# Stick-breaking stage of a two-layer decoder trunk: TensorE in program order, longer step distances, an output projection begun with one half of its inputs

## The chip, the cores and the metric

The kernel runs on one core of one Trainium2 chip. The time is the device time of one execution in microseconds (us), the median of several runs. The kernel before takes 1203.66 us (three runs, 1200.4 to 1204.41).

## The reference

`x` is 256 tokens of 1024 features in float32. Two layers each do four updates of `x`: a half-weighted SwiGLU, a token mixer, cross-attention into 256 memory tokens, and a second half-weighted SwiGLU, each behind an RMS norm. The mixer of the even layer has two kinds of heads whose outputs are concatenated and projected:

```
x = x + 0.5 * swiglu_ffn(rms_norm(x, ...), ...)
h = rms_norm(x, mix_norm[layer])
x = x + even_mixer(h, ...)      # layer 0:  [banded heads | stick-breaking heads] @ w_out
x = x + odd_mixer(h, ...)       # layer 1
x = x + memory_cross_attention(rms_norm(x, ...), rms_norm(mem, ...), ...)
x = x + 0.5 * swiglu_ffn(rms_norm(x, ...), ...)
```

Stick-breaking attention, for each of 8 heads of 64 features, over keys `s` before token `t`:

```
z = q . k * dh**-0.5
log_keep  = where(strict, log_sigmoid(-z), 0)
log_after = cumsum(log_keep, reverse) - log_keep
a = where(strict, exp(log_sigmoid(z) + log_after), 0)
o = a @ v
```

## The kernel before, in words

Nearly all of the work is float32 matrix products, each made as three products of float32r parts: an operand is split into a high part and the rest, and `mm3` (lines 182 to 184) issues high x high, high x low and low x high. A weight tile (128 x 1024) is loaded by SyncE's queue into one of 4 buffers `raw`; ScalarE casts it to `wh` (line 175), VectorE subtracts to `wl` (line 177), 10 buffers of each. `project` (line 266) makes a product with 1024 output features: for the first 128 tokens (t = 0) it runs over the 8 slices k of the weights with both column halves c, then for t = 1 over c and k. One `step` of it is one `mm3` of 512 columns, so three matmuls, and calls `tick(650)`.

Small work is put between those steps by hand. `later(delay, fn, tag)` puts a function into a heap with a due time on a planning clock (in ns, line 92); every `tick` advances the clock and then calls at most one function that is due; `need(tag)` (line 108) calls functions in order of due time until none with that tag is left. The delays stand in the table `LAG` (line 30). The recorded program is then given to a list scheduler, which sets the order on each engine by a cost model of its own, except under `tc.manual_schedule(engines=...)`, where the engines named keep the order of the program.

Around the change, in `even_mixer` (line 547): after the banded heads, `mem.keys()` (a `project` of the memory tokens) runs on TensorE, and the steps of the stick-breaking heads are meant to stand between its matmuls. For head h:

- `stick` (line 699): for each second head the scores of two heads (lines 705 and 708, 64 rows of the array each), masks (713, VectorE); then ScalarE 716, 717, 718, VectorE 722, ScalarE 724 (high part), VectorE 725 (low part) and 727.
- `after` (732), due `stick_u` later: three matmuls that make the running sums (734 with the high part, 735 with the low part, 736), called a triple below; then VectorE 738, ScalarE 739.
- `values` (746), due `stick_v` later, for two heads: four groups of matmuls of line 496. After heads 3 and 7 a split (line 190 on ScalarE, 191 on VectorE) puts the outputs into `xh`, `xl`, the left operand of the output projection.

`need("stick")` then empties the heap, and the last `project` (line 772) multiplies by `w_out`. Its slices k = 0 to 3 need the banded heads alone, k = 4, 5 heads 0 to 3 and k = 6, 7 heads 4 to 7. `head256` (519) makes normed, transposed queries and keys of the cross-attention, with a transpose (`tp`, line 212) due `head256` after the scaling (452 or 536). In the cross-attention `attend` scales the probabilities (452) and has them transposed `x_p` later.

Of the kernel before, what the change touches and what calls it, by code (L numbers as in the profile page):

```python
# [18 lines left out]
P = 128  # L19
S = 256  # L20
D = 1024
NK = D // P
# [5 lines left out]


LAG = {  # L30
    "norm": 5000, "silu": 5000, "pv": 3000, "head256": 2200, "band": 7500, "band_gap": 2600, "band_p": 7500,
    "put": 400, "att_norm": 4500, "band_norm": 3500, "stick_gap": 1900, "stick_u": 3200, "stick_v": 1000, "stick_o": 1300, "head64": 7000,
    "att_first": 3800, "att_gap": 3300, "att_p": 17600, "att_o": 1800, "x_s": 18000, "x_p": 4000, "x_out": 3600,
    "mem_e": 5400, "mem_o": 4600, "rs64": 2700, "rs256": 1900, "rsband": 6100,
}

# [2 lines left out]
def kernel(  # L39
# [52 lines left out]
    def later(delay, fn, tag=None):  # L92
        serial[0] += 1
        heapq.heappush(heap, (clock[0] + delay, serial[0], tag, fn))
# [8 lines left out]
    def tick(ns):  # L103
        clock[0] += ns
        if heap and not busy[0] and heap[0][0] <= clock[0]:
            dispatch()

    def need(tag):
        while any(e[2] == tag for e in heap):
            dispatch()  # L110
# [32 lines left out]
    xh, xl = xs[:, 0], xs[:, 1]  # L143
# [22 lines left out]
    def weights(src, r=None, kept=False):  # L166
        if r is None:
            r = raw.tile([P, 1024], F32, name="raw")
        if len(src.shape) == 4:
            for g in range(2):  # L170
                nc.sync.dma_start(r.rearrange("p (k g n) -> p k g n", g=2, n=src.shape[3])[:, :, g, :], src[:, :, g, :])
        else:
            (kept_load if kept else nc.sync.dma_start)(r if len(src.shape) == 2 else blocks(r, src.shape[2]), src)
        wh = wsp.tile([P, 1024], F32R, name="wh")
        nc.scalar.copy(wh, r)  # L175
        wl = wsp.tile([P, 1024], F32R, name="wl")
        nc.vector.tensor_tensor(wl, r, f32(wh), op=ALU.subtract)  # L177
        return wh, wl
# [10 lines left out]
    def split_to(dh, dl, src):  # L189
        nc.scalar.copy(dh, src)  # L190
        nc.vector.tensor_tensor(dl, src, f32(dh), op=ALU.subtract)  # L191
# [45 lines left out]
    def announce(vec, kept=False):  # L237
        upcoming["gain"] = None if vec is None else load_gain(vec, kept)
# [11 lines left out]
    def add_to_x(scale):  # L250
        def evac(t, c, ps):
            xs = xres[t][:, c * 512:(c + 1) * 512]
            if scale == 1.0:
                nc.vector.tensor_tensor(xs, ps, xs, op=ALU.add)
            else:
                nc.vector.scalar_tensor_tensor(xs, in0=ps, scalar=scale, in1=xs, op0=ALU.mult, op1=ALU.add)
            x_updated(t, c)
        return evac
# [4 lines left out]
    def xboth(k):  # L263
        return xh[:, :, k, :], xl[:, :, k, :]

    def project(view, lhs, evac, nk=NK, tags=(None, None)):

        head = nk - 8
        ps = [[None, None], [None, None]]

        def step(t, c, k, w):
            if k == 0:
                ps[t][c] = psum()
            mm3(ps[t][c], lhs(t, k), cols(w, c * 512, 512), k == 0, k == nk - 1)
            tick(650)

        for k in range(head):
            w = weights(view(k))
            for t in range(2):
                for c in range(2):  # L280
                    step(t, c, k, w)
        if tags[0]:
            need(tags[0])
        ws = []
        for k in range(head, nk):
            ws.append(weights(view(k)))
            for c in range(2):
                step(0, c, k, ws[-1])
        for c in range(2):
            evac(0, c, ps[0][c])  # L290
        if tags[1]:
            need(tags[1])
        for c in range(2):
            for k in range(head, nk):
                step(1, c, k, ws[k - head])
            evac(1, c, ps[1][c])
# [250 lines left out]
    def even_mixer(w_in, q_gain, k_gain, sinks, w_out, next_vec, mem, first=False):  # L547
# [141 lines left out]
        need("band")  # L689

        for t in range(2):
            later(LAG['put'] + 1000 * t, lambda t=t: split_to(xh[:, t, 0:4, :], xl[:, t, 0:4, :], oA[:, t]), f"o{t}")

        po = [None]

# [3 lines left out]
        def stick(h):  # L699
            b = h // 2  # L700
            if h % 2 == 0:
                two = [psum(), psum()]
                rows = [slice(0, 64), slice(64, 128)]
                for ps, hs in zip(two, rows):
                    nc.tensor.matmul(ps.rearrange("p (a t) -> p a t", t=256)[:, :, 0:128],  # L705
                                     lhsT=kbT[hs, b, 0:P], rhs=qbT[hs, b, :], start=True, stop=False)
                for ps, hs in zip(two, rows):
                    nc.tensor.matmul(ps[:, 128:256], lhsT=kbT[hs, b, P:2 * P], rhs=qbT[hs, b, P:2 * P],
                                     start=False, stop=True)
                tick(800)  # L710
                for i in range(2):
                    zs[i] = work()
                    nc.vector.tensor_tensor(zs[i][:, 0:384], two[i][:, 0:384], smask, op=ALU.add)  # L713
            z = zs[h % 2][:, 0:384]
            e = work()
            nc.scalar.activation(e[:, 0:384], z, AF.Abs)
            nc.scalar.activation(e[:, 0:384], e[:, 0:384], AF.Exp, scale=-1.0)
            nc.scalar.activation(e[:, 0:384], e[:, 0:384], AF.Ln, bias=1.0)
            sp = work()
            sph = work(F32R)  # L720
            spl = work(F32R)
            nc.vector.scalar_tensor_tensor(sp[:, 0:384], in0=z, scalar=0.0, in1=e[:, 0:384],
                                           op0=ALU.max, op1=ALU.add)
            nc.scalar.copy(sph[:, 0:384], sp[:, 0:384])
            nc.vector.tensor_tensor(spl[:, 0:384], sp[:, 0:384], f32(sph[:, 0:384]), op=ALU.subtract)
            a = work()
            nc.vector.scalar_tensor_tensor(a[:, 0:384], in0=z, scalar=0.0, in1=e[:, 0:384],
                                           op0=ALU.min, op1=ALU.subtract)
            if h < 7:
                later(LAG['stick_gap'], lambda: stick(h + 1), "stick")  # L730

            def after():
                pc = psum()
                nc.tensor.matmul(pc[:, 0:384], lhsT=neg_ur, rhs=sph[:, 0:384], start=True, stop=False)
                nc.tensor.matmul(pc[:, 0:384], lhsT=neg_ur, rhs=spl[:, 0:384], start=False, stop=False)
                nc.tensor.matmul(pc[:, 256:384], lhsT=neg_1, rhs=sp[:, 128:256], start=False, stop=True)
                tick(540)
                nc.vector.tensor_tensor(a[:, 0:384], pc[:, 0:384], a[:, 0:384], op=ALU.add)
                nc.scalar.activation(a[:, 0:384], a[:, 0:384], AF.Exp)

                weighed[h % 2] = a.rearrange("p (b n) -> p b n", n=P)
                if h % 2 == 0:
                    return
                both = list(weighed)

                def values():
                    if h % 4 == 1:
                        po[0] = blocks(psum())
                    b = (h // 2) % 2
                    pair = (h - 1, h)  # L750

                    def vs(kb):
                        return lambda g: vb[:, kb, g * 64:(g + 1) * 64]
                    value_pairs(lambda g: po[0][:, 2 * b:2 * b + 2, :], pair, vs(0),
                                lambda g: both[g % 2][:, 0:3:2, :], True, False)
                    value_pairs(lambda g: po[0][:, 2 * b + 1, :], pair, vs(1),
                                lambda g: both[g % 2][:, 1, :], False, True)
                    tick(660)
                    if h % 4 == 3:
                        o = po[0]  # L760
                        b4 = 4 + 2 * (h // 4)
                        later(LAG['stick_o'], lambda: split_to(
                            *[x[:, :, b4:b4 + 2, :].rearrange("p t f n -> p f t n") for x in (xh, xl)],
                            o.rearrange("p (f t) n -> p f t n", f=2)), "o0")
                later(LAG['stick_v'], values, "stick")
            later(LAG['stick_u'], after, "stick")

        later(0, lambda: stick(0), "stick")
        mem.keys()
        need("stick")  # L770
        announce(next_vec)
        project(lambda k: w_out[k * P:(k + 1) * P, :], xparts, add_to_x(1.0), tags=("o0", "o1"))


    def odd_mixer(w_in, q_gain, k_gain, w_out, next_vec, mem):
# [278 lines left out]
```

## Time and profile before

| | us |
|---|---|
| median of three runs | 1203.66 |
| the profiled execution | 1202.92 |
| its span, first to last instruction | 1201.2 |
| TensorE busy, 99% of the span | 1189.3 |
| VectorE busy, 65% | 775.1 |
| ScalarE busy, 54% | 646.5 |

TensorE is busy nearly all the time, and 93% of the chain that ended last is its own. A matmul's busy time is longer than its turn in the queue, because matmuls overlap; what one costs is the distance from its start to the start of the next. In the timeline the first column is the start in us from the start of the span, the second the time until the end of the last of the merged instructions.

### The profile page before, as it was taken

What the parts mean: (1) busy time and instruction counts of PE and PEld (TensorE: products, weight loads), DVE (VectorE), ACT (ScalarE), POOL (GpSimd) and SP (SyncE); (2) the same over time, 40 slices, a digit from 0 to 9 for tenths busy, and PEclk for the clock granted to TensorE, in tenths of its full rate; (3) what the DMA queues carried; (4) which work ended last, traced back from release to release, by engine and by line L of the source; (5) the groups of instructions that cost most, each with busy time, mean ns of one, the idle gap of its engine ahead of it and who ended that gap; (6) DMA issues with size and microseconds to landing.
All of it is one profiled execution on the core that took longest, in us unless ns stands there. A gap on an engine that the chain in (4) does not pass through costs nothing.

```text
span 1201.2 us, 16964 instructions
## 1 busy us (share of the span) xinstructions
PE 1189.3 (99%) x6320; PEld 998.7 (83%) x6320; DVE 775.1 (65%) x1026; ACT 646.5 (54%) x1080; POOL 63.9 (5%) x123
## 2 busy tenths in 40 slices
PE   8999999999999999999999999999999999999998
PEld 7888888986788888888888888888777888888887
DVE  6766645696777676665375765376786676667651
ACT  6656534665565466555265564265764564655540
POOL 1000000200110000000000000032000100000000
PEclk9999999999999999999999999999999999999999
DMA  8865674731454485666376657445753645665560
GB/s 253 255 195 172 218 223 131 258 105 53 145 167 144 153 266 172 191 209 210 108 250 189 193 181 274 141 158 167 230 169 121 210 143 160 202 205 188 182 192 35
DMA packets 136756, 216.70 MB, mean 180 GB/s; under 512 B 10337, under 2 KB 104161, under 8 KB 136674
## 3 DMA queue, kind: packets, MB, share of 16 engines
q1 hardware_dynamic: 136674, 215.63, 55.4%
q8 instruction: 49, 0.80, 0.3%
q14 instruction: 33, 0.27, 0.1%
HBM read 214.54 MB, written 1.05 MB: 179 GB/s over the span
## 4 chain that ended last, share of the span: by engine, by line
PE 93%; DVE 3%; DMA 2%; ACT 1%; issue 1%; POOL 0%; SPq 0%; ACTq 0%; POOLq 0%; DVEq 0%
PE mm L323 23%; PE mm L182 17%; PE mm L184 17%; PE mm L183 17%; PE mm L324 12%; PE tp L212 3%; PE mm L496 1%; DVE wl L177 1%; DMA raw<-in_xa_w_o_dram 1%; DMA raw<-in_ffn_w_gu_dram 1%; ACT wh L175 1%; PE mm L305 1%; PE mm L841 1%; DVE big L191 0%; PE mm L705 0%
## 5 line engine op out<-in xcount | busy, mean ns | idle before, releaser
L177 DVE TENSOR_TENSOR wl<-raw,wh 128x1024 fp32r<-128x1024 f32 x386 | 463.9, 1220 | 145.4 <-ACT wh L175 142.5
L175 ACT CAST wh<-raw 128x1024 fp32r<-128x1024 f32 x386 | 394.3, 1051 | 156.9 <-PE mm L184 78.7
L323 PE MATMUL mm<-xs,wh 128*128 128x512 f32 x1184 | 413.7, 394 | 0.0
L324 PE MATMUL mm<-xs,wl 128*128 128x256 f32 x1184 | 331.8, 280 | 0.0
L323 PEld LDWEIGHTS mm<-xs,wh 128*128 128x128 f32 x1184 | 221.7, 187 | 50.3
L324 PEld LDWEIGHTS mm<-xs,wl 128*128 128x128 f32 x1184 | 223.8, 189 | 0.0
L182 PE MATMUL mm<-wh,big 128*128 128x512 f32 x480 | 191.3, 399 | 0.3 <-DVE wk L713 0.3
L184 PE MATMUL mm<-wh,big 128*128 128x512 f32 x480 | 188.4, 392 | 0.0
L183 PE MATMUL mm<-wl,big 128*128 128x512 f32 x480 | 188.2, 392 | 0.0
L182 PE MATMUL mm<-wh,xs 128*128 128x512 f32 (+1 forms) x432 | 171.7, 398 | 0.0
L184 PE MATMUL mm<-wh,xs 128*128 128x512 f32 (+1 forms) x432 | 167.1, 387 | 0.0
L183 PE MATMUL mm<-wl,xs 128*128 128x512 f32 (+1 forms) x432 | 167.0, 386 | 0.0
L327 ACT COPY wk<-mm 128x256 f32<-128x256 f32 x148 | 55.0, 372 | 147.1 <-PE mm L324 146.7
L328 DVE TENSOR_TENSOR wk<-mm,wk 128x256 f32<-128x256 f32 x148 | 62.1, 421 | 94.7 <-ACT wk L327 94.7
L182 PEld LDWEIGHTS mm<-wh,big 128*128 128x128 f32 x480 | 90.5, 188 | 20.3 <-issue 2.4
L184 PEld LDWEIGHTS mm<-wh,big 128*128 128x128 f32 x480 | 90.4, 188 | 19.3 <-issue 0.3
L183 PEld LDWEIGHTS mm<-wl,big 128*128 128x128 f32 x480 | 90.6, 189 | 17.4 <-issue 0.2
L184 PEld LDWEIGHTS mm<-wh,xs 128*128 128x128 f32 x432 | 81.1, 188 | 16.9 <-issue 0.2
L182 PEld LDWEIGHTS mm<-wh,xs 128*128 128x128 f32 x432 | 81.3, 188 | 15.0 <-issue 0.5
L183 PEld LDWEIGHTS mm<-wl,xs 128*128 128x128 f32 x432 | 81.4, 188 | 14.5 <-issue 0.2
L212 PE MATMUL tp<-ident,wk 128*128 128x128 f32 x352 | 52.9, 274 | 2.4 <-DVE wk L452 0.8
L212 PEld LDWEIGHTS tp<-ident,wk 128*128 128x128 f32 x352 | 42.1, 140 | 14.2 <-issue 2.3
(148 smaller groups left out, 921.6 us busy)
## 6 DMA issues: line engine op xcount, KB each, us to landing
raw<-in_ffn_w_gu_dram SPq DMA_DIRECT2D x344, 256.0 KB, 4.2
raw<-in_ffn_w_down_dram SPq DMA_DIRECT2D x88, 512.0 KB, 4.5
raw<-in_xa_w_kv_dram SPq DMA_DIRECT2D x32, 512.0 KB, 5.4
raw<-in_od_w_in_dram SPq DMA_DIRECT2D x24, 512.0 KB, 4.5
raw<-in_ev_w_in_dram SPq DMA_DIRECT2D x18, 512.0 KB, 4.7
raw<-in_xa_w_q_dram SPq DMA_DIRECT2D x16, 512.0 KB, 4.2
raw<-in_xa_w_o_dram SPq DMA_DIRECT2D x16, 512.0 KB, 4.4
raw<-in_ev_w_out_dram SPq DMA_DIRECT2D x8, 512.0 KB, 4.1
```

Source lines behind the costliest of these rows:

```text
L175: nc.scalar.copy(wh, r)
L177: nc.vector.tensor_tensor(wl, r, f32(wh), op=ALU.subtract)
L182: nc.tensor.matmul(ps, lhsT=a[0], rhs=b[0], start=start, stop=False)
L183: nc.tensor.matmul(ps, lhsT=a[0], rhs=b[1], start=False, stop=False)
L184: nc.tensor.matmul(ps, lhsT=a[1], rhs=b[0], start=False, stop=stop)
L212: nc.tensor.transpose(ps[:, b * P:(b + 1) * P], src[:, b * P:(b + 1) * P], ident)
L305: nc.tensor.matmul(ps[:, b * 256:(b + 1) * 256], lhsT=w[k // per][x][:, o:o + P], rhs=xboth(k)[y], start=i == 0 and k == 0, stop=i == 2 an ...
L323: nc.tensor.matmul(ps, lhsT=wh, rhs=xs[:, :, :, k, :], start=k == 0, stop=False)
L324: nc.tensor.matmul(ps[:, 0:256], lhsT=wl, rhs=xh[:, :, k, :], start=False, stop=k == NK - 1)
L327: nc.scalar.copy(part[:, bs], ps[:, 256:512])
L328: nc.vector.tensor_tensor(out[:, bs], ps[:, 0:256], part[:, bs], op=ALU.add)
L496: nc.tensor.matmul(dst(h)[rows], lhsT=lhs(h), rhs=rhs(h), start=first, stop=last)
```

## The change

Three parts. The table of delays: `silu` 5000 to 8000, `head256` 2200 to 3600, `stick_gap` 1900 to 2400, `stick_u` 3200 to 4000, `stick_v` 1000 to 2200, `x_p` 4000 to 5000, and the tick of a triple 540 to 680. `project` gets `early`: the `need` of its first tag is called before slice `head + early`, not before the first. And the stage itself, from the first stick-breaking step to the end of the output projection, is recorded with TensorE in program order; before it needs only the tag "band", and the last stick-breaking steps may stand between the first steps of the output projection.

```diff
-    "norm": 5000, "silu": 5000, "pv": 3000, "head256": 2200, ...
-    ... "stick_gap": 1900, "stick_u": 3200, "stick_v": 1000, "stick_o": 1300, "head64": 7000,
-    ... "x_s": 18000, "x_p": 4000, "x_out": 3600,
+    "norm": 5000, "silu": 8000, "pv": 3000, "head256": 3600, ...
+    ... "stick_gap": 2400, "stick_u": 4000, "stick_v": 2200, "stick_o": 1300, "head64": 7000,
+    ... "x_s": 18000, "x_p": 5000, "x_out": 3600,
...
-    def project(view, lhs, evac, nk=NK, tags=(None, None)):
+    def project(view, lhs, evac, nk=NK, tags=(None, None), early=0):
...
-        if tags[0]:
-            need(tags[0])
         ws = []
         for k in range(head, nk):
+            if k == head + early and tags[0]:
+                need(tags[0])
             ws.append(weights(view(k)))
...
-            later(LAG['put'] + 1000 * t, lambda t=t: split_to(...), f"o{t}")
+            later(LAG['put'] + 1000 * t, lambda t=t: split_to(...), "band")
...
-                tick(540)
+                tick(680)
...
-                            o.rearrange("p (f t) n -> p f t n", f=2)), "o0")
+                            o.rearrange("p (f t) n -> p f t n", f=2)), "stick")
...
-        later(0, lambda: stick(0), "stick")
-        mem.keys()
-        need("stick")
-        announce(next_vec)
-        project(lambda k: w_out[k * P:(k + 1) * P, :], xparts, add_to_x(1.0), tags=("o0", "o1"))
+        with tc.manual_schedule(engines={mybir.EngineType.PE}):
+            later(0, lambda: stick(0), "stick")
+            mem.keys()
+            need("band")
+            announce(next_vec)
+            project(lambda k: w_out[k * P:(k + 1) * P, :], xparts, add_to_x(1.0), tags=("stick", None), early=4)
```

The lines of the changed kernel stand one or two further down; line 734 of before is line 735 there.

What stands on TensorE before the kernel's change at head 6 of the stick-breaking heads (its triple 734 to 736, the values of heads 4 and 5, two transposes of the memory keys; `mm<-wh,big` and `mm<-wl,big` are matmuls of the memory keys' projection):

```order
L182 MATMUL mm<-wh,big 128x512
L734 MATMUL mm<-wk,neg_ur 128x384
L183 MATMUL mm<-wl,big 128x512
L184 MATMUL mm<-wh,big 128x512
L735 MATMUL mm<-wk,neg_ur 128x384
L736 MATMUL mm<-wk,neg_101 128x128
L496 MATMUL mm<-wk,big 64x256 x2
L496 MATMUL mm<-wk,big 64x128
L212 MATMUL tp<-ident,wk 128x128 x4
L496 MATMUL mm<-wk,big 64x128
L182 MATMUL mm<-wh,big 128x512
```

The same place of the changed kernel, from the triple of head 6 on:

```order
L735 MATMUL mm<-wk,neg_ur 128x384
L736 MATMUL mm<-wk,neg_ur 128x384
L737 MATMUL mm<-wk,neg_101 128x128
L182 MATMUL mm<-wh,big 128x512
L183 MATMUL mm<-wl,big 128x512
L184 MATMUL mm<-wh,big 128x512
L497 MATMUL mm<-wk,big 64x256 x2
L497 MATMUL mm<-wk,big 64x128 x2
```

Triples, pairs of scores and groups of values are split by other matmuls before, and stand whole after. Between the triples of heads 5 and 6 there are 13 matmuls of the projection before and 9 after.

ScalarE before the change, heads 6 and 7 (716 to 718 and 724 of head 6 on wk_2980 and wk_2985; 739 of head 5 on wk_2930; casts of `w_out` are wh_3148 and wh_3167, L525 squares of the memory keys):

```order
L716 ACTIVATE wk_2980<-wk_2976 128x384
L717 ACTIVATE wk_2980<-wk_2980 128x384
L525 ACTIVATE junk_3030,ssx_3029<-mm_2950 128x256
L718 ACTIVATE wk_2980<-wk_2980 128x384
L739 ACTIVATE wk_2930<-wk_2930 128x384
L525 ACTIVATE junk_3032,ssx_3029<-mm_2950 128x256
L724 CAST wk_2985<-wk_2984 128x384
L175 CAST wh_3148<-raw_3146 128x1024
L175 CAST wh_3167<-raw_3165 128x1024
```

The same in the changed kernel (head 6 on wk_3006 and wk_3011, 739 of head 5 on wk_2965, the casts wh_3144 to wh_3205 of `w_out`):

```order
L175 CAST wh_3144<-raw_3142 128x1024
L717 ACTIVATE wk_3006<-wk_3002 128x384
L190 CAST big_2699<-tp_3036 128x4x128
L718 ACTIVATE wk_3006<-wk_3006 128x384
L175 CAST wh_3160<-raw_3158 128x1024
L719 ACTIVATE wk_3006<-wk_3006 128x384
L740 ACTIVATE wk_2965<-wk_2965 128x384
L175 CAST wh_3181<-raw_3179 128x1024
L175 CAST wh_3193<-raw_3191 128x1024
L725 CAST wk_3011<-wk_3010 128x384
L175 CAST wh_3205<-raw_3203 128x1024
```

Four casts of `w_out` stand ahead of head 6's copy (724, now 725), where before none did.

VectorE in the changed kernel at head 6 (722 on wk_3010 and 725 on wk_3012, `wl` the low parts of `w_out`):

```order
L739 TENSOR_TENSOR wk_2965<-mm_3046,wk_2965 128x384
L177 TENSOR_TENSOR wl_3162<-raw_3158,wh_3160 128x1024
L723 SCALAR_TENSOR_TENSOR wk_3010<-wk_3002,wk_3006 128x384
L177 TENSOR_TENSOR wl_3183<-raw_3179,wh_3181 128x1024
L177 TENSOR_TENSOR wl_3195<-raw_3191,wh_3193 128x1024
L726 TENSOR_TENSOR wk_3012<-wk_3010,wk_3011 128x384
```

Two low parts stand between 722 and 725 of head 6; before, 725 followed 722 directly there.

## Rows read from the trace of the kernel before

**Rows 1.** Page, part 1: busy us, share of the span, instructions.
```profile
PE 1189.3 (99%) x6320; PEld 998.7 (83%) x6320; DVE 775.1 (65%) x1026; ACT 646.5 (54%) x1080; POOL 63.9 (5%) x123
```
**Rows 2.** Who TensorE waited for: total us, times, longest.
```profile
PE mm L734 <- ACT wk L724: 0.9, 1, 0.9
PE tp L212 <- DVE wk L452: 0.8, 2, 0.6
...
PE mm L496 <- DVE wk L481: 0.6, 1, 0.6
PE tp L212 <- DVE wk L481: 0.4, 1, 0.4
```
**Rows 3.** Stretches: us, busy us (instructions) of each engine, granted clock, DMA.
```profile
273.70:329.80 56.10, 54.42 (x249) 39.59 (x248) 37.58 (x61) 33.15 (x71) 5.07 (x11) 0.97 0.29 95
286.00:290.30 4.30, 2.62 (x11) 1.48 (x10) 2.72 (x7) 1.97 (x5) 0.55 (x1) 1.00 0.00 0
290.30:293.70 3.40, 3.40 (x10) 2.23 (x10) 1.93 (x4) 1.97 (x4) 0.00 (x0) 0.50 0.02 5
```
**Rows 4.** Timeline, TensorE, 297 to 317 us: start, us, line, count.
```profile
297.50 0.70 PE L705 MATMUL mm<-big 64*128 64x256 f32 x2
...
298.34 0.50 PE L183 MATMUL mm<-wl,big 128*128 128x512 f32 x1
...
300.32 0.33 PE L734 MATMUL mm<-wk,neg_ur 128*128 128x384 f32 x1
...
300.81 0.48 PE L182 MATMUL mm<-wh,big 128*128 128x512 f32 x1
301.12 0.39 PE L183 MATMUL mm<-wl,big 128*128 128x512 f32 x1
301.36 0.40 PE L184 MATMUL mm<-wh,big 128*128 128x512 f32 x1
...
315.56 0.87 PE L496 MATMUL mm<-wk,big 128*64 128x256 f32 x6
316.35 0.66 PE L212 MATMUL tp<-ident,wk 128*128 128x128 f32 x4
316.76 0.48 PE L182 MATMUL mm<-wh,xs 128*128 128x512 f32 x1
```
**Rows 5.** Timeline, 273 to 275 us: head 0's high and low part, TensorE.
```profile
273.44 0.39 PE L184 MATMUL mm<-wh,big 128*128 128x512 f32 x1
...
273.94 0.51 ACT L724 CAST wk<-wk 128x384 fp32r<-128x384 f32 x1 [0.62 <-DVE wk L722]
...
274.49 0.56 DVE L725 TENSOR_TENSOR wk<-wk 128x384 fp32r<-128x384 f32 x1
```
**Rows 6.** Groups by line, 270 to 318 us: busy us, mean ns.
```profile
L175 ACT CAST wh<-raw 128x1024 fp32r<-128x1024 f32 x7 | 7.2, 1047 | 1.1 <-DMA raw<-in_ev_w_out_dram 1.1
...
L190 ACT CAST big<-tp 128x512 fp32r<-128x512 f32 x4 | 2.3, 585 | 0.0
...
L177 DVE TENSOR_TENSOR wl<-raw,wh 128x1024 fp32r<-128x1024 f32 x7 | 8.3, 1215 | 0.0
L725 DVE TENSOR_TENSOR wk<-wk 128x384 fp32r<-128x384 f32 x8 | 4.5, 557 | 4.1 <-ACT wk L724 4.1
```
**Rows 7.** Timeline: two low parts free weight buffers, a cast waits for one's load.
```profile
306.50 2.35 DVE L177 TENSOR_TENSOR wl<-raw,wh 128x1024 fp32r<-128x1024 f32 x2
...
313.56 1.05 ACT L175 CAST wh<-raw 128x1024 fp32r<-128x1024 f32 x1 [1.07 <-DMA raw<-in_ev_w_out_dram]
```
**Rows 8.** Timeline, TensorE, second cross-attention: a wait at a transpose.
```profile
967.31 0.39 PE L184 MATMUL mm<-wh,big 128*128 128x512 f32 x1
968.29 0.63 PE L212 MATMUL tp<-ident,wk 128*128 128x128 f32 x4 [0.60 <-DVE wk L452]
```
**Rows 9.** Timeline, start of the kernel: first weight cast, first matmuls.
```profile
10.49 1.04 ACT L175 CAST wh<-raw 128x1024 fp32r<-128x1024 f32 x1 [0.73 <-DMA raw<-in_ffn_w_gu_dram]
...
12.08 1.22 PE L305 MATMUL mm<-xs,wh 128*128 128x256 f32 x4 [0.61 <-ACT xs L190]
```

More of the change, by code (lines that the diff above doesn't have):

```diff
@@ L30 @@
 LAG = {
-    "norm": 5000, "silu": 5000, "pv": 3000, "head256": 2200, "band": 7500, "band_gap": 2600, "band_p": 7500,
-    "put": 400, "att_norm": 4500, "band_norm": 3500, "stick_gap": 1900, "stick_u": 3200, "stick_v": 1000, "stick_o": 1300, "head64": 7000,
-    "att_first": 3800, "att_gap": 3300, "att_p": 17600, "att_o": 1800, "x_s": 18000, "x_p": 4000, "x_out": 3600,
+    "norm": 5000, "silu": 8000, "pv": 3000, "head256": 3600, "band": 7500, "band_gap": 2600, "band_p": 7500,
+    "put": 400, "att_norm": 4500, "band_norm": 3500, "stick_gap": 2400, "stick_u": 4000, "stick_v": 2200, "stick_o": 1300, "head64": 7000,
+    "att_first": 3800, "att_gap": 3300, "att_p": 17600, "att_o": 1800, "x_s": 18000, "x_p": 5000, "x_out": 3600,
     "mem_e": 5400, "mem_o": 4600, "rs64": 2700, "rs256": 1900, "rsband": 6100,
@@ L691, in even_mixer @@
         for t in range(2):
-            later(LAG['put'] + 1000 * t, lambda t=t: split_to(xh[:, t, 0:4, :], xl[:, t, 0:4, :], oA[:, t]), f"o{t}")
+            later(LAG['put'] + 1000 * t, lambda t=t: split_to(xh[:, t, 0:4, :], xl[:, t, 0:4, :], oA[:, t]), "band")
         po = [None]
```

## The prediction

> **What bounds the kernel now.** The page's busy times come first: TensorE (PE) is busy 1189.3 us, 99% of the span [rows 1], so only what TensorE itself does, or waits for, can move the time. Next I read who TensorE waited for: the list is short, and its largest entry inside the program is one wait of 0.9 us at line 734 [rows 2]. A stage whose engine hardly waits can still be slow in two ways, and the table of stretches shows one: in the changed stage the clock was granted at 1.2 of 2.4 GHz for 3.4 us, right after a stretch of 4.3 us in which TensorE was busy for 2.62 us [rows 3]. The other way is how the matmuls stand to each other, and that is read from distances of starts in the timeline [rows 4].
>
> I take the stretch from 273.7 to 329.8 us, 56.1 us [rows 3], which holds the same work in both kernels: 72 matmuls of the memory keys, 72 of `w_out`, 8 triples, three pairs of scores, four groups of values, four blocks of transposes. From the timeline [rows 4]: a matmul of 512 columns takes 0.23 (301.12 to 301.36); a triple that stands whole 0.49 (300.32 to 300.81), and it slows the matmul behind it from 0.23 to 0.31, so 0.57; whole scores 0.84 (297.50 to 298.34) and about 0.2 for their neighbours, 1.04; whole values 0.79 (315.56 to 316.35) and 0.2, 0.99; a block of transposes 0.41 (316.35 to 316.76), 0.44 with its neighbour. Sum without any wait: 144 x 0.23 + 8 x 0.57 + 3 x 1.04 + 4 x 0.99 + 4 x 0.44 = 33.1 + 4.6 + 3.1 + 4.0 + 1.8 = 46.6 us. So the kernel before spends 9.5 us above that: 1.7 for 3.4 us at half clock, 1.7 idle in the stretch before it (4.30 less 2.62 [rows 3]), and the remainder, near 6, because the small groups are cut apart and every change between 64 and 128 rows or columns costs again.
>
> **The change part by part.** *Program order on TensorE* puts the groups together, and the stretch would fall by the whole 9.5 us if nothing waited. But a matmul whose input is late now holds up all that stands behind it; before, other matmuls had been put in between. So for each triple I compare when TensorE reaches it with when its inputs are ready. I find four waits.
>
> Head 0. Ten matmuls stand ahead of the triple now, not 17; the tenth starts at 273.44, so TensorE arrives at 273.67. The order on ScalarE and VectorE up to there is unchanged, so the high part is ready at 274.45 and the low part at 275.05 [rows 5]. With hand-over the triple's second matmul starts near 275.1 where it would have started at 273.85: 1.3 us.
>
> Head 3. Its running sums take the memory buffer in which scores of head 4 lie, and these are released by the mask (713) of head 4, which VectorE does behind head 3's 725 and 727. Adding 0.5 to 0.6 per step along that chain I get about 0.9 us.
>
> Head 6. Call T the issue of head 5's triple. TensorE then has 9 matmuls and arrives at T + 0.5 + 9 x 0.23 = T + 2.6. ScalarE has, in its new order, the second activation of head 6, a cast, the third activation, 739 of head 5, two casts and only then the copy of the high part (724). Casts are 1.05 each [rows 6], the others 0.5 [rows 5]; what stands ahead of them ends near T + 0.35, since it includes a copy (190, 0.6 [rows 6]) of a transpose that TensorE makes about 1.2 us before T. So the high part is ready at T + 0.35 + 3 x 1.05 + 3 x 0.45 = T + 4.9. On VectorE the low parts of the last two casts stand ahead of 725: they are 1.2 each [rows 6] and begin when the first of these casts is done, T + 3.5, so 725 (0.56) ends at T + 6.4. Wait: 2.4 for the first matmul of the triple, 1.2 for the second, 3.6 us in all.
>
> Head 7. Call U the issue of the second matmul of head 6. TensorE arrives at the triple at U + 4.1 (six matmuls of the keys, values, transposes, three of `w_out`). On ScalarE the high part stands behind a copy of those same transposes (done at U + 3.6), two short squares and one more cast: U + 3.6 + 0.4 + 0.6 + 0.4 + 1.05 + 0.5 = U + 6.4; the low part waits for 1.2 of VectorE more and 0.56 for itself, U + 7.6. Wait 3.4 us.
>
> Sum of waits 9.2 us, so 46.6 + 9.2 = 55.8 against 56.1. The waits at heads 6 and 7 are at least as long as the stretch of little work that came before the slow clock [rows 3]; I take one slow spell of 3.4 us, fully paid, 1.7 us (bounds 0 and 3.4). The stage: +1.4 us. No row shows a triple that waits for a cast in ScalarE's queue, so the bounds of the waits are 1.7 us (what it idles now [rows 3]) and 12 (each chain half a us longer, one load late).
>
> The Trainium skill, "TensorE: Matmul & The Clock Gate", section "HAM oscillation — how this bites in real kernels", describes waits between groups of matmuls after each of which TensorE goes on at the low clock. By it both long waits would be followed by a spell, and 3.4 us of slow clock would stand in place of 1.7. The trace agrees with it at its one stall, and it is a rival below.
>
> *The early start of the output projection* I cost at nothing: in the timeline matmuls of `w_out` already stand between the last steps (316.76 follows the last values [rows 4]), because the scheduler before had put them there. The left operands of heads 4 to 7 are needed 21 matmuls (some 5 us) after the last values and take one copy and one subtraction, 1.3 us; if that cover were gone, 1 us.
>
> *`x_p`, 4000 to 5000.* In each cross-attention one transpose waits for scaled probabilities: in the second it starts 0.98 after the matmul before it, not 0.23 [rows 8], and the two waits sum to 0.8 us idle [rows 2], so the first loses about 0.4. Now each comes three matmuls (0.7 us) later: 0.75 + 0.4 = 1.1 us gained. Bounds 0 and 1.2.
>
> *`silu` and `head256`* move transposes by some steps where TensorE did not wait: nothing, hidden by the projections around them, whose results are needed tens of us later. In the odd layer's mixer the transposes of the keys now fall otherwise between attention steps that already wait twice for 481 (0.6 and 0.4 [rows 2]); I take 0, bounds -1 and +1.
>
> *SyncE's queue.* The load of `gq` (128 x 256 floats replicated, 128 KB) moves from the middle of the program to the front, ahead of the first weight load. There the first cast waits for its load 0.73 us and the first matmuls for ScalarE behind it [rows 9], so a delay goes to the end. A weight load of 512 KB was there 4.7 us after its buffer came free (308.85 to 313.56 [rows 7]); 128 KB at that rate are 1.2 us, the upper bound, and 0 if they pass beside the loads of `x`. I take 0.3.
>
> Sum: +1.4 - 1.1 + 0.3 = +0.6 us. The profiled execution took 1202.92 us (1201.2 of span and 1.7 around it), 0.06% below the median of the runs shown; 1202.92 + 0.6 = 1203.5 us.
>
> **Rivals.** First, the waits at heads 6 and 7 are mostly absent: 3.6 + 3.4 + 1.7 us go, and the time is 1203.5 - 8.7 = 1194.8; with one of them gone, 1199. For it: by the list a single triple waited before [rows 2]. Against: the order on ScalarE and VectorE is fixed, and the four casts stand ahead of head 6's copy whatever TensorE does. 0.28.
>
> Second, slower: the cast of the last `w_out` slice stands ahead of all of head 7 on ScalarE, and it needs a load that can only start when a low part frees its buffer. Before, it began 4.7 us after that (308.85 to 313.56), having waited 1.07 us for the load, with nothing behind it that TensorE wanted soon [rows 7]. Now the buffer comes free at about T + 2.7, the load at T + 7.4, and head 7 has about 0.6 us to spare behind it; from there each us that the load is late is a us at the end. A load late by 3 us costs 2.4 and makes the wait at head 7 so long that a second slow spell follows, 1.7: 1203.5 + 4.1 = 1207.6. 0.16.
>
> Third, two slow spells without that: 1203.5 + 1.7 = 1205.2. This is what the page named above would give. Both waits are alike, which speaks for it; that the first spell may pass in part while TensorE waits anyway speaks against it. 0.16.
>
> The forecast itself, 0.40.
>
> **How the numbers follow.** What a measurement of this kernel can tell from no change is 0.3%, 3.6 us: below 1200.05 is faster, above 1207.3 slower. Faster: the first rival, and a small tail of the forecast, 0.30. Slower: the second, 0.16. Within: the rest, 0.54. The range from 1196 to 1207.8 leaves out the first rival at its full price and what lies above the second.
>
> **What the changed profile would show.** That the groups come together: triples in one piece at 0.5 us, and the sum of the stretch without waits near 46.6. The waits: TensorE's list names 734 and 735 (now 735 and 736) against ScalarE 724 and VectorE 725 with some 8 us, and two gaps of over 2 us near 300 and 308 us. The clock: a slow stretch behind one of them. The cross-attention: no wait of 0.6 at the transpose. I am wrong if the list of waits has less than 4 us there (then faster), if the stretch without its waits is far from 46.6, or if ScalarE waits over 2 us for a `w_out` load ahead of head 7 (then slower).

## The result, and the profile after

| | before | after |
|---|---|---|
| median of six runs each, us | 1202.12 (1200.40 to 1204.41) | 1208.85 (1207.34 to 1209.55) |
| ratio | | 1.0054, 95% interval 1.0043 to 1.0065 |
| span of the profiled execution | 1201.2 | 1207.1 |

The changed kernel is 0.54% slower, 6.7 us; 1203.5 was predicted. The page's row of busy times and its row of the granted clock, for the changed kernel (most lines carry a number one higher than before: 734 is 735 now, 724 is 725):

```profile
PE 1188.8 (98%) x6320; PEld 998.7 (83%) x6320; DVE 775.3 (64%) x1026; ACT 647.3 (54%) x1080; POOL 63.3 (5%) x123
...
PEclk9999999999799999999999999999999999999999
```
TensorE is as long busy as before [rows 1] and the span is 5.9 us longer; one slice, from 302 to 332 us, has the clock at 7 tenths. Who TensorE waited for, in the changed kernel (in all, times, longest):

```profile
PE mm L735 <- ACT wk L725: 4.4, 3, 2.1
...
PE mm L736 <- DVE wk L726: 2.1, 3, 1.1
...
PE tp L212 <- DVE wk L231: 1.0, 1, 1.0
...
PE mm L735 <- DVE wk L714: 0.8, 1, 0.8
```
Against [rows 2]: the waits at the triples that were forecast are there, and the wait of the transpose for the scaled probabilities (452) is gone. One at the transposes of a norm (231) is new at 1.0 us. Heads 0, 3, 6 and 7 in the timeline of TensorE (start, us, line, and in brackets the idle time before and its releaser):

```profile
274.45 0.44 PE L735 MATMUL mm<-wk,neg_ur 128*128 128x384 f32 x1 [0.68 <-ACT wk L725]
275.05 0.45 PE L736 MATMUL mm<-wk,neg_ur 128*128 128x384 f32 x1 [0.15 <-DVE wk L726]
...
287.05 0.41 PE L735 MATMUL mm<-wk,neg_ur 128*128 128x384 f32 x1 [0.82 <-DVE wk L714]
...
300.56 0.39 PE L184 MATMUL mm<-wh,big 128*128 128x512 f32 x1
303.00 0.44 PE L735 MATMUL mm<-wk,neg_ur 128*128 128x384 f32 x1 [2.05 <-ACT wk L725]
304.50 0.69 PE L736 MATMUL mm<-wk,neg_ur 128*128 128x384 f32 x1 [1.06 <-DVE wk L726]
...
313.01 0.44 PE L735 MATMUL mm<-wk,neg_ur 128*128 128x384 f32 x1 [1.69 <-ACT wk L725]
314.33 0.69 PE L736 MATMUL mm<-wk,neg_ur 128*128 128x384 f32 x1 [0.88 <-DVE wk L726]
```
And what ScalarE and VectorE do at head 6:

```profile
300.55 1.98 ACT L175 CAST wh<-raw 128x1024 fp32r<-128x1024 f32 x2
301.62 2.36 DVE L177 TENSOR_TENSOR wl<-raw,wh 128x1024 fp32r<-128x1024 f32 x2
302.43 0.52 ACT L725 CAST wk<-wk 128x384 fp32r<-128x384 f32 x1
...
303.90 0.55 DVE L726 TENSOR_TENSOR wk<-wk 128x384 fp32r<-128x384 f32 x1
```
Two casts of weights stand ahead of head 6's high part, two low parts ahead of its low part, as worked out. From start to start the waits take 8.7 us (1.2 at head 0, 1.0 at head 3, 3.5 at head 6, 3.0 at head 7) where 9.2 were forecast. The stretch itself, then the two pieces at half clock, each behind the stretch that precedes it (us, busy us and instructions by engine, granted clock):

```profile
273.70:334.85 61.15, 53.81 (x250) 40.19 (x250) 37.93 (x61) 33.40 (x71) 5.00 (x11) 0.89 0.27 85
299.00:303.40 4.40, 2.35 (x10) 1.45 (x8) 4.33 (x6) 4.40 (x7) 0.00 (x0) 1.00 0.65 179
303.47:310.29 6.82, 5.79 (x20) 3.94 (x21) 5.34 (x8) 3.54 (x8) 0.00 (x0) 0.50 0.81 254
310.29:313.70 3.41, 1.48 (x7) 0.73 (x5) 1.81 (x2) 3.22 (x8) 0.92 (x2) 1.00 0.49 171
313.70:320.53 6.83, 6.20 (x17) 4.58 (x17) 3.33 (x6) 0.73 (x2) 0.00 (x0) 0.50 0.55 154
```
The work of 56.1 us [rows 3] takes 61.15. Where the forecast has one spell of 3.4 us at half clock there are two of 6.8; in them matmuls of 512 columns start 0.43 us apart instead of 0.23. Ahead of each TensorE was busy for about half the time (2.35 of 4.40 us, 1.48 of 3.41).

That is 5.1 of the 5.9 us. The rest lies elsewhere, and the first part of it had been costed at nothing. The wide pairs of the SwiGLUs (now 324 and 325) were not looked at before. First and last wide matmul of layer 0's second SwiGLU, 288 pairs, in the kernel before:

```profile
443.08 0.48 PE L323 MATMUL mm<-xs,wh 128*128 128x512 f32 x1
...
542.99 0.39 PE L323 MATMUL mm<-xs,wh 128*128 128x512 f32 x1
```
and in the changed kernel:

```profile
448.17 0.39 PE L324 MATMUL mm<-xs,wh 128*128 128x512 f32 x1
...
549.92 0.40 PE L324 MATMUL mm<-xs,wh 128*128 128x512 f32 x1
```
99.91 us against 101.75, with nothing idle in between and the clock full. The pairs follow each other either at 347 ns or at 353 (on average 346.7 and 353.3). Before, the first 15 of each later SwiGLU run at 353, then come two transposes (397), and the other 273 run at 347. With `silu` at 8000 transposes stand behind the 9th and the 24th pair. The starts of pairs 11, 24 and 26 of this SwiGLU in the changed kernel:

```profile
451.91 0.40 PE L324 MATMUL mm<-xs,wh 128*128 128x512 f32 x1
...
456.43 0.39 PE L324 MATMUL mm<-xs,wh 128*128 128x512 f32 x1
...
457.35 0.40 PE L324 MATMUL mm<-xs,wh 128*128 128x512 f32 x1
```
Between the two breaks 13 pairs take 4.52 us, 348 ns each; behind the second, 262 take 92.57 us (457.35 to 549.92), 353 each. In the two SwiGLUs of layer 1 this profile has the last 264 at 347; whether that is the rule was open.

### The profile page after: what moved, and what is told of

Same layout as the page of the kernel before. It is cut to its first block, busy times and chain, and to the rows that moved or that the text cites. A ratio compares the mean times of both kernels' runs of the same rounds, so it can differ in the third digit from the quotient of the medians.

```text
span 1207.1 us, 16966 instructions
## 1 busy us (share of the span) xinstructions
PE 1188.8 (98%) x6320; PEld 998.7 (83%) x6320; DVE 775.3 (64%) x1026; ACT 647.3 (54%) x1080; POOL 63.3 (5%) x123
## 4 chain that ended last, share of the span: by engine, by line
PE 94%; ACT 2%; DVE 2%; DMA 1%; issue 1%; POOL 0%; SPq 0%; ACTq 0%; DVEq 0%; POOLq 0%
PE mm L324 23%; PE mm L182 18%; PE mm L183 18%; PE mm L184 18%; PE mm L325 12%; PE tp L212 3%; ACT wh L175 1%; PE mm L497 1%; DMA raw<-in_ffn_w_gu_dram 1%; DVE wl L177 1%; PE mm L306 1%; PE mm L843 0%; DMA x<-in_x_dram 0%; PE tp L398 0%; DVE wk L616 0%
```

## The experiments

All were timed beside the kernel before; the ratio is to its runs at that time. The stage's length is taken in each trace from the start of the 219th matmul of line 183 to that of the 273rd. "At 353" counts, of the three later SwiGLUs, those whose long stretch of pairs runs at 353 ns.

| kernel | median, us | ratio, 95% interval | stage, us | of it at half clock | at 353 |
|---|---|---|---|---|---|
| before | 1202.1 to 1202.7 | 1 | 62.06 | 3.4 | 0 |
| changed | 1208.85 | 1.0054 (1.0043 to 1.0065) | 67.16 | 13.7 | 1 |
| e1_list_order | 1205.25 | 1.0018 (1.0007 to 1.0028) | 63.18 | 6.8 | 3 |
| e2_program_order_only | 1202.85 | 0.9998 (0.9986 to 1.0011) | 59.99 | 0 | 0 |
| e3_filler | 1208.41 | 1.0032 (1.0019 to 1.0045) | 61.77 | 0 | 3 |
| e4_other_delays | 1205.26 | 1.0022 (1.0011 to 1.0033) | 61.97 | 3.4 | 3 |
| f1_changed_again | 1209.70 | 1.0060 (1.0043 to 1.0076) | 63.30 | 3.4 | 3 |
| f2_silu_back | 1206.09 | 1.0027 (1.0014 to 1.0041) | 67.15 | 13.6 | 0 |
| f3_filler_silu_back | 1202.62 | 1.0003 (0.9991 to 1.0014) | 61.78 | 0 | 0 |
| f4_late_triples | 1196.90 | 0.9955 (0.9943 to 0.9968) | 56.76 | 0 | 0 |
| g1_silu_only | 1205.86 | 1.0026 (1.0014 to 1.0039) | 60.51 | 0 | 3 |
| g2_break_in_first | 1196.09 | 0.9950 (0.9935 to 0.9965) | 56.74 | 0 | 0 |
| g3_break_in_later | 1202.09 | 0.9993 (0.9982 to 1.0004) | 56.75 | 0 | in part |
| g4_both | 1196.08 | 0.9952 (0.9935 to 0.9968) | 55.83 | 0 | 0 |

**First group.** Theory A said that the waits and the clock in the stage make the loss, theory B that the longer distances and the other delays do.

e1, the list scheduler orders the stage again:

```
-        with tc.manual_schedule(engines={mybir.EngineType.PE}):
-            later(0, lambda: stick(0), "stick")
...
+        later(0, lambda: stick(0), "stick")
...
```


> The changed kernel with one part undone: the stage is again left to the list scheduler; all step distances, the early start of the output projection and the other delays stay. Theory A (TensorE in program order waits 8.6 us at the triples, and the clock that falls behind two of these waits costs 6 more, while the groups in one piece give back 9.5): without program order waits, slow clock and gain all go, the stage is back at 56 to 57 us, and with 1.1 from x_p the kernel takes about 1201 us (1200 to 1203), some 7.5 below the changed kernel. Theory B (the longer distances, the early start and the other delays make the loss, whoever orders TensorE): 1206 to 1210, no lower than the changed kernel by more than 2 us.

1205.25: neither. One wait of TensorE in the stage, and the stretch behind it:

```profile
PE mm L735 <- DVE wl L177: 2.4, 1, 2.4
```
```profile
304.94:311.76 6.82, 6.68 (x23) 4.86 (x24) 4.50 (x8) 3.39 (x8) 1.65 (x2) 0.50 0.70 241
```
A wait behind a late low part in VectorE's queue, and 6.8 us at half clock after it, come without program order too: the stage is 1.1 us longer than before. The three later SwiGLUs, all at 353, add 5.5.

e2, program order alone, on the kernel before:

```
-        later(0, lambda: stick(0), "stick")
...
+        with tc.manual_schedule(engines={mybir.EngineType.PE}):
+            later(0, lambda: stick(0), "stick")
...
```


> The kernel before with one part of the change: TensorE keeps the order of the program in the stage; the step distances and delays are those of before, the output projection begins once all heads are done. Theory A: every triple now comes one to three steps (0.7 to 2 us) sooner than in the changed kernel, so the waits grow: 10 to 16 us of waits at the triples, at least two slow spells; 1207 to 1214 us. Theory B (program order is harmless, the longer distances cost): the groups in one piece give their 9 us back and the kernel takes 1195 to 1199.

No change that can be measured, 1202.85; both theories miss. In the profile the stage is 2.1 us shorter, with 5.2 us of waits in it (the longest 2.05 us, at head 0) and the clock full. With the old distances ScalarE and VectorE were given another order, in which no long wait stands at heads 6 and 7. My expectation carried the waits of one queue order over to another.

e3, work put into the waits:

```
                 pc = psum()
+                for _ in range(14 if h >= 6 else 0):
+                    nc.tensor.matmul(pc[:, 0:128], lhsT=neg_1, rhs=ident, start=True, stop=True)
```


> The changed kernel with work added: ahead of the triples of heads 6 and 7 TensorE makes 14 matmuls of 128 columns each in float32 (about 3 us each time), whose result the triple overwrites; the waits there are 3.1 and 2.6 us long, so the added work should lie inside them. Theory A (the clock falls because TensorE idles there, and it costs 6 us): the clock stays up, and the kernel takes 1203 us (1202 to 1205.5) with more work. Theory C (the waits alone make the loss, or the clock does not set the time there): the time stays at 1208.5 or rises by up to 1 us, 1208 to 1210.

By the median alone theory C won: 1208.41; the ratio, 1.0032 for 1.0054, is 0.2% below that of the changed kernel. The trace says more. The whole stage:

```profile
269.49:331.26 61.77, 59.87 (x340) 47.44 (x339) 43.43 (x68) 35.68 (x77) 5.00 (x11) 1.00 0.29 94
```
The clock stays up, and the stage falls from 67.16 to 61.77: 5.4 us for the clock. But in this profile all three later SwiGLUs ran at 353, not one (3.4 us), it lost 1.2 us more in its first 150 us, and a wait for 231 between the layers cost 1.4: the gain did not reach the end.

e4, only the delays outside the stage:

```
-    "norm": 5000, "silu": 5000, "pv": 3000, "head256": 2200, ...
+    "norm": 5000, "silu": 8000, "pv": 3000, "head256": 3600, ...
```
(and `x_p` 5000)

> The kernel before with the delays outside the stage alone changed (silu 8000, head256 3600, x_p 5000); the stick-breaking stage is as before. Theory A: x_p removes two waits at transposes, 1.1 us, the others nothing: 1201 us (1200 to 1202.5), within what can be told from no change. Theory B: these delays carry part of the loss (a slower pace in the second SwiGLU of layer 0, the start): 1203.5 to 1206.

1205.26, theory B's range. The stage is as before, the three later SwiGLUs run at 353. So theory A was half of it, and a theory D for the other half was put to the test: `silu` sets the pace of the wide pairs.

**Second group.** f1 is the changed kernel once more.

> The changed kernel once more, beside the three that follow. Theory A (clock): 13 to 14 us of half clock in the stage again, the stage near 61 us. Theory D (a second loss: the wide pairs of matmuls of the later SwiGLUs, lines 324 and 325, run at 347 ns a pair or at 353, and with silu 8000 the transposes fall so that the long stretch of 264 pairs runs at 353): at least one of the three later SwiGLUs at 353, as in the first profile, 1.7 us each. The time about 1208.5 (1207 to 1210).

1209.70, but by another way. The stage of this profile, the part ahead of the slow clock and the slow part:

```profile
274.00:334.00 60.00, 52.67 (x261) 39.33 (x262) 40.18 (x64) 35.30 (x75) 4.98 (x11) 0.97 0.29 94
```
```profile
303.90:307.97 4.07, 1.17 (x5) 0.89 (x6) 3.99 (x6) 2.92 (x5) 0.00 (x0) 1.00 0.83 215
307.97:311.38 3.41, 3.41 (x13) 1.94 (x12) 3.41 (x5) 2.63 (x5) 0.00 (x0) 0.50 0.76 276
```
The waits at heads 6 and 7 are the same to 0.01 us (2.05, 1.06, 1.70, 0.88), yet only one spell of 3.4 us follows, and the stage is 1.2 us longer than before, close to the +1.4 forecast. All three later SwiGLUs run at 353 instead. The page's row of the wide matmul, here 399 ns against 394 before the change, shows it at a glance:

```profile
L324 PE MATMUL mm<-xs,wh 128*128 128x512 f32 x1184 | 419.0, 399 | 0.0
```

f2 takes `silu` back:

```
-    "norm": 5000, "silu": 8000, ...
+    "norm": 5000, "silu": 5000, ...
```


> The changed kernel with silu back at 5000, nothing else. By theory D the transposes stand once and not twice among the wide pairs of each later SwiGLU, and the long stretch goes back to 347 ns a pair: 1.7 us less for each of the three that ran at 353; 1204.5 (1203 to 1206.5). If the delay of silu does not set the pace (rival: the pace is chance, from run to run), the time stays at 1208.5, and the profile shows a mixture of both paces in the long stretches.

1206.09, 3.6 us less, and the same row:

```profile
L324 PE MATMUL mm<-xs,wh 128*128 128x512 f32 x1184 | 413.7, 394 | 0.0
```
All three long stretches are at 347. Theory D's size fits; this profile has two spells of 6.8 us in its stage.

f3, that and the added work of e3:

> Both together: the added work ahead of the triples of heads 6 and 7, and silu at 5000. If theories A and D are both right and their losses add: 5.4 less for the clock and up to 5 less for the pace, of which the changed kernel shows not all in each run; 1200.5 (1199 to 1202.5), below the kernel before by the 2 us that the cross-attention and the odd mixer give. If only D: 1204 to 1206; if only A: 1203 to 1204.

1202.62, another 3.5 us less. With `silu` 8000 the same work had moved the median by 0.4 us and the ratio by 0.2%, so that the two losses simply add is not shown. It is 2 us above what I expected, level with the kernel before. In its trace the stage is 0.3 us shorter than before and the pace that of before, but 1.5 us go in the first 150 us and 1.8 at one wait for 231 between the layers (1.6 idle), which I had not counted; neither stands in every profile.

f4, the triples of heads 6 and 7 placed where their inputs are ready:

```
-            later(LAG['stick_u'], after, "stick")
+            later(LAG['stick_u'] + {6: 4600, 7: 3950}.get(h, 0), after, "stick")
...
-            project(..., tags=("stick", None), early=4)
+            project(..., tags=("stick", None), early=6)
```
(`silu` 5000)

> The changed kernel with silu at 5000 and, instead of added work, with the triples of heads 6 and 7 placed later (stick_u + 4600 and + 3950), so that matmuls of the keys and of w_out stand where TensorE waited; the output projection may run six slices instead of four before it needs the heads. If the waits and the clock behind them are what the stage lost, both go: stage 46.6 + 1.7 (heads 0 and 3) + up to 1 = 48 to 50 us against 56.1; 1194.5 (1193 to 1197). Rival: the order on ScalarE and VectorE makes other waits (a late load of w_out ahead of head 7), 1198 to 1202.

1196.90, 0.45% faster than before. Its waits in the stage, and the two triples:

```profile
PE tp L212 <- DVE wk L453: 1.6, 1, 1.6
PE mm L735 <- DVE wk L714: 0.8, 1, 0.8
PE mm L735 <- ACT wk L725: 0.7, 1, 0.7
```
```profile
306.98 0.34 PE L735 MATMUL mm<-wk,neg_ur 128*128 128x384 f32 x1
307.16 0.34 PE L736 MATMUL mm<-wk,neg_ur 128*128 128x384 f32 x1
...
310.99 0.33 PE L735 MATMUL mm<-wk,neg_ur 128*128 128x384 f32 x1
311.16 0.34 PE L736 MATMUL mm<-wk,neg_ur 128*128 128x384 f32 x1
```
Heads 6 and 7 wait for nothing and no slow clock follows. f2, with the waits, is 9.2 us above f4. What the grouped order gives was there all along. The stage is 5.3 us shorter than before, so 50.8 us for the 56.1 where 48 to 50 were expected: the wait that is left at a transpose (1.6) is what that range did not hold. The later triples and the six slices were not tried apart.

**Third group.** Does a break among the wide pairs set their pace? g1, `silu` 8000 in the kernel before and nothing else:

> The kernel before with silu 8000 and nothing else. Theory D (where the transposes stand among the wide pairs sets their pace): in each of the three later SwiGLUs 264 of 288 pairs at 353 ns, +1.75 us each, so 5.2 if all three, 1.75 if one; 1205 to 1207.5. Rival (the loss of the other delays lies in head256 or x_p): the time of before, 1202 (1201 to 1203).

1205.86: the delay alone costs 3.2 us; e4, with `head256` and `x_p` changed too, took 1205.26, so these are not needed for it. All three long stretches are at 353, and each of these SwiGLUs is 1.8 us longer in the trace. By chance this profile has no slow clock in its stage, though each engine's order there and the waits ahead of the spell of [rows 3] (0.36, 0.90 and 0.27 us) are those of before, and the stage is 1.55 us shorter: that is what the one spell cost.

g2 adds a break in the first SwiGLU, g3 one in each later SwiGLU:

```
                 nc.tensor.matmul(ps[:, 0:256], lhsT=wl, ...)
+                wide[0] += 1
+                if wide[0] in (13,):        # g3: (320 + 125, 608 + 125, 896 + 125)
+                    pt = tps()
+                    for _ in range(2):
+                        nc.tensor.transpose(pt[:, 0:P], part[:, 0:P], ident)
```


> The kernel with late triples and silu 5000, and with work added: two transposes of 128 columns behind the 13th wide pair of the first SwiGLU, whose result nothing uses; in every profile so far its 320 pairs ran at 353 ns without a break. Theory D: the transposes switch the pace to 347, 307 x 6.3 ns = 1.9 us less for 0.15 us of added work: 1195.1 (1194.3 to 1196). Rival (the pace does not hang on such a break): 1197, 0.15 more than without.

> The same kernel with the two added transposes in each of the three later SwiGLUs instead, 163 pairs before their end, where the pairs run at 347. Theory D in its simple form (each such break switches the pace): the last 163 pairs at 353, 1.0 us each and 0.15 for the transposes: +3.5, 1200.4 (1199.5 to 1201.5). Rival (a break can only hasten, or does nothing): 1197.4.

g2: 1196.09, and the interval says no more than "as f4". Wide matmuls (326) in 100 us of its first SwiGLU, behind the break (second column, in brackets):

```profile
34.00:134.00 100.00, 100.00 (x284) 53.18 (x284) 1.00 0.64 204
```
Still 353; theory D in its simple form fails here. g3, 35 us ahead of the break in layer 0's second SwiGLU and 35 us behind it:

```profile
445.00:480.00 35.00, 35.00 (x102) 18.88 (x102) 1.00 0.61 185
485.00:520.00 35.00, 35.00 (x100) 18.64 (x100) 1.00 0.60 182
```
The break did switch it, from 347 to 353; so it did in layer 1's first SwiGLU, and in the last one, which here began at 347 and had turned to 353, back to 347. 1202.09 is 5.2 above f4 where 3.5 were expected; in the trace the three SwiGLUs are 3.5 us longer.

g4 joins g2's break with head 0's triple one step later (`{0: 650, 6: 4600, 7: 3950}`):

> Late triples, silu 5000, the added transposes in the first SwiGLU, and the triple of head 0 one step later (stick_u + 650), where TensorE waited 0.7 us: 1.9 - 0.15 + 0.7 less than the late triples alone, 1194.4 (1193.3 to 1195.5). If the break does nothing: 1196.3.

The median, 1196.08, is that of g2 and not below f4 by what can be told. Its profiled execution took 1193.88, and there the same break did switch the first SwiGLU:

```profile
33.00:133.00 100.00, 100.00 (x290) 54.02 (x289) 1.00 0.67 213
```
The same two transposes at the same place gave 353 in one execution and 347 in the other. The stage is 0.9 us shorter than f4's.

## Why the prediction was wrong

**Waits, grouping: right.** TensorE's order, the four waits and the engines behind them came as worked out; 8.7 us of waits for 9.2. Taking the waits and 6.0 us of clock off the stretch leaves 61.15 - 8.7 - 6.0 = 46.5 us for the grouped work, forecast 46.6. The 6.0 are the two slow stretches less what their matmuls take at 0.23 apart; by the stage of e3 they are 5.4, and the grouped work 47.1. With the clock full on both sides the changed stage is some 61.8 (67.16 less 5.4) against 60.5 (g1): +1.3, where the forecast without clock is 55.8 - (56.1 - 1.7) = +1.4. The first rival, no waits, was wrong for the change as it stands, but f2 to f4, 9.2 us, bears out its price of 8.7.

**First failed step: "`silu` and `head256` move transposes by some steps where TensorE did not wait: nothing".** I looked for waits alone. The transposes of `silu` 8000 fall among the wide pairs twice instead of once, and behind them 264 pairs of each later SwiGLU run 6.6 ns slower, 1.7 us a time. Shown by taking it back (f2, -3.6 us) and by doing it alone (g1, +3.2 us): half of the loss. In the profiles, 16 of 18 long stretches with `silu` 8000 ran at 353 (six profiles), and of 21 with 5000 none (seven profiles, g3 left out). The traces also show how two breaks differ from one: of the 65 breaks of two transposes among wide pairs in the fourteen traces, 63 left the other of the two paces behind them. One break turns 353 to 347 for the rest of a SwiGLU; a second turns it back. The two stretches that stayed at 347 belong to SwiGLUs that began at 347; the two breaks that changed nothing are the first in e1's last SwiGLU and that of g2. Three SwiGLUs at 353 are 5.5 us in a trace; that medians moved by 3.2 to 3.6 may be since not every execution has three, as the first profile of the changed kernel had one. A timed run without a trace does not show this.

**Second, a term mis-sized: "one slow spell of 3.4 us, fully paid, 1.7 us (bounds 0 and 3.4)".** Two spells of 6.8 us cost 5.4 to 6.0 in the changed kernel's profile and stood again in f2; in f1 one of 3.4. So 1.7 was one of the outcomes, and the upper bound was too low: it took the length of a spell from the only one in the trace. Filling the waits (f2 to f3) gave 3.5 us back, the other half of the loss. The mean granted clock of the timed executions goes the same way: 0.9955, 0.9962 and 0.9953 for the changed kernel, f1 and f2 (17 in all), 0.9991 and 0.9993 for e3 and f3 (23), which from f2 to f3 is some 9 us less at half clock. That the clock is all of the 3.5 us is not shown: one execution of f2 had 0.999 and still took 1204.93, above f3's median of 1202.62. The third rival had the second spell and its place, but at 1.7 us. The Trainium skill, "TensorE: Matmul & The Clock Gate", section "HAM oscillation — how this bites in real kernels", has TensorE go on at the low clock after each wait between its groups of matmuls, waits of 3 to 5 us for a DMA. Here single waits are 0.88 to 2.05 us; the first profile of the changed kernel agrees at both long waits, its second profile, with the same waits, at one only, and g1, with the waits of before, at none.

**The rest held.** The cross-attention gained 0.5 and 0.9 us in the changed kernel's trace (forecast 1.1 in all). The odd mixer moved by -0.2 (0 ± 1). The load of `gq` at the front: the first 150 us took 0.06 us less and 2.7 more than before in two profiles of the same kernel, so 0.3 can't be told from chance. What differs is the clock at the start: the first wide pair begins at 24.3 us in e4, where the clock is full from 10.4 us on, at 26.3 before (from 17.2), at 28.9 in f1 (from 21.3). The second rival, a late load ahead of head 7, did not come: the cast waited 0.95 us for its load (304.84), behind head 6's high part, and nothing at head 7 waited for it beyond the forecast. The early start of the output projection was not run by itself. What remains of the sum, f3, is level with before.

## What to carry to other kernels

Where instructions are moved into a dense stretch of another engine's work, count the breaks and look at the distances of starts on both sides of each in the profile, not for waits alone: a change of 6.6 ns in a pair that runs 264 times is 1.7 us. When the order of one engine is fixed, place each step by when its inputs come out of the other engines' queues as they then are (f4), since a wait costs itself and may cost a slower clock on top. A slow spell seen once gives neither its length nor its count for the next kernel; profile the kernel twice before a cause is settled on a time alone.

## What the runs showed of the hardware that was not expected

- Two paces of one instruction sequence, 347 and 353 ns for a matmul of 512 columns and one of 256, at full clock and with no wait, each holding for as long as nothing else stands between. Two transposes of 128 columns switched it, either way, in 63 of 65 cases; behind the 13th pair of the first SwiGLU in one of two executions. Why two cases did not, and what sets the pace with which a SwiGLU begins, is open.
- Slow spells behind the same waits were 6.8 us twice, or 3.4 us once, in executions of the same program. A single wait of 2.05 us (e2) or 1.56 us (f4) was followed by none, one of 2.40 us (e1) by 6.8 us.
- Small float32 matmuls, 14 ahead of each late triple (3.3 us), kept the clock at full through the stage (e3, f3). But g1, with the stage's order and waits of before, has no spell either where the kernel before has one of 3.4 us: the clock is not decided by the program alone.
